# Hybrid attention and MLP trunk on one core: keys and queries split two heads at once, their halves placed by transfers inside SBUF

## The chip, the cores and the metric

The kernel runs on one core of a Trainium2 chip. Its engines work side by side, each through its own list of instructions in order: TensorE (PE, matmuls and transposes), VectorE (DVE), ScalarE (ACT), GpSimd (POOL), and SyncE (SP), which issues all transfers (DMAs) of this kernel. The metric is the time of one execution on the device in microseconds (us), as the median of several runs.

## What is computed

Two layers (DEPTH = 2) on x of 512 rows and 1024 columns, in float32. Each layer projects the normalised x once and hands the parts to three groups of attention heads of width 64; their outputs go through one output projection, and a gated MLP with a short causal convolution follows. Cut to what the change touches:

```python
FOX_HEADS, NSA_HEADS, NSA_KV_GROUPS, DIL_HEADS, HEAD_DIM = 4, 8, 2, 4, 64
proj = h @ w_in
(fq, fk, fv, ff, nq, kc, vc, ks, vs, kw, vw, ng, dq, dk, dv) = jnp.split(proj, splits, axis=-1)
o_fox = fox_attention(heads(fq, 4), heads(fk, 4), heads(fv, 4), log_f)
o_nsa = nsa_attention(rope(nq, 8), rope(kc, 2), heads(vc, 2), rope(ks, 2), heads(vs, 2),
                      rope(kw, 2), heads(vw, 2), gates, ...)
o_dil = dilated_attention(rope(dq, 4), rope(dk, 4), heads(dv, 4))
mix = concatenate([o_fox, o_nsa, o_dil], axis=-1);  return mix @ w_out
# within each: s = einsum('bqhd,bkhd->bhqk', q, k) * 64 ** -0.5, masked softmax, times v
```

## The kernel before

**Numbers.** A float32 value goes into PE as two parts in the format F32R: `hi`, the rounded value, and `lo`, the rest. A product is hi·hi + hi·lo + lo·hi. ACT writes hi (a copy into an F32R tile), DVE writes lo (value minus hi).

**Layout of scores.** A head has 64 columns, the array 128 rows. A tile `q` [128, 2 heads, 512 positions] holds for each head hi in partitions 0 to 63 and lo in 64 to 127. A tile `k` [128, 2, 512] belongs to one head: `k[:, 0]` holds hi twice, in both halves of the partitions, `k[:, 1]` lo twice. So two matmuls over 128 partitions make a score block from all parts.

**How they come about.** A projection leaves 128 positions x 64 columns per head in PSUM. `staged(...).evac` (L717 on) brings each of four position blocks into a row tile `r` (with `rope`, which rotates 16 of the 64 columns); for keys (`dup`) it writes every head twice side by side. `turn` (L735) turns a 128-column strip of the four row tiles with four PE transposes into one PSUM tile `pt` of [128, 512]: for queries two heads above each other, for keys one head twice. One step later `keep` calls the split: `q_evac` (ACT L485, DVE L486, once per head, 64 partitions each) or `k_evac` (ACT L492, DVE L493, 128 partitions, once per head). For the forgetting heads' keys `fk` the turning (`t_block`, L476) and the split stand in one line of their own. `fq` needs no turning: its split reads the projection's accumulator.

**Stages of a layer.** fq, fk, fv are projected first; then 96 attention units run (16 of the group f, 64 of n, 16 of d), and between them pieces of the other projections: nq (8 heads in two halves, nq0 and nq1), ks and kw (2 heads each, nks and nkw), kc and vc for the compressed keys, dq, dk, dv. The order on PE is written out by hand in program order: each unit's nine stages lie a fixed number of units apart (`LAGS`), `step()` issues the next piece, `budget` spreads the pieces over the units, and `operands(u)` calls `until(...)`, which issues pieces until the unit's q and k exist. The other engines' lists are ordered by a scheduler. Weights come through `load` (L134, SP) into one of few `raw` buffers per weight and are split by ACT (L148) and by DVE or POOL (L150).

**Buffers.** Row tiles `r` come from a pool of 10, q and k from a pool of 24 (`b`). PSUM has 2 buffers `pt`, 3 `acc`, 2 `s`, 1 `o`: a `pt` is free for the next transposes when both split operations have read it.

Of the kernel before, what the change touches and what calls it, by code (L numbers as in the profile page):

```python
# [10 lines left out]
F32R = mybir.dt.float32r  # L11
I32 = mybir.dt.int32
AF = mybir.ActivationFunctionType
ALU = mybir.AluOpType
# [60 lines left out]
def tile_hybrid_block(  # L75
# [6 lines left out]
    nc = tc.nc  # L82
# [12 lines left out]
    def nm(p):  # L95
        uid[0] += 1
        return f"{p}_{uid[0]}"

    def ps(tag):
        return psum.tile([128, 512], F32, tag=tag, bufs=PSB[tag], name=nm(tag))  # L100

    def bt(shape, dt=F32, name="b"):
        return big.tile(shape, dt, tag="b", name=nm(name))

    def rt(shape=(128, 512), dt=F32):
        return rowp.tile(list(shape), dt, tag="r", name=nm("r"))
# [4 lines left out]
    def f(ap):  # L111
        return ap.bitcast(F32)
# [4 lines left out]
    def bc(ap, axis, n):  # L117
        a = ap.unsqueeze(axis)
        shape = list(a.shape)
        shape[axis] = n  # L120
        return a.to_broadcast(shape)
# [322 lines left out]
    for l in range(DEPTH):  # L444
# [5 lines left out]
        def s_mms(o, s, ks, w, first, last):  # L450
            sl = slice(128 * s, 128 * s + 128)
            n = len(ks)
            ks = list(ks)
            order = sorted(range(n), key=lambda i: KORDER.index(ks[i]))
            for z, i in enumerate(order):
                k, i = ks[order[z]], order[z]
                mm(o, HH(k)[:, sl], w[0][:, i], first and z == 0, False)
                mm(o, HH(k)[:, sl], w[1][:, i], False, False)
                mm(o, HL(k)[:, sl], w[0][:, i], False, last and z == n - 1)
# [15 lines left out]
        def t_block(tiles, c0):  # L475
            p = ps("pt")  # L476
            for s in range(NST):
                nc.tensor.transpose(p[:, 128 * s:128 * s + 128], tiles[s][:, c0:c0 + 128], ident)
            return p
# [8 lines left out]
            return q  # L488

        def k_evac(p):  # L490
            k = bt([128, 2, 512], F32R, "k")
            nc.scalar.activation(k[:, 0, :], p, AF.Copy)  # L492
            nc.vector.tensor_sub(k[:, 1, :], p, f(k[:, 0, :]))  # L493
            return k

        def new_v(nh=2):
            return bt([128, 8 // nh, nh, 2, 64], F32R, "v")
# [6 lines left out]
        def hd(ap):  # L504
            return ap.rearrange("p (h d) -> p h d", d=64)

        store = {}
        sl256 = lambda pp, s: pp[s // 2][:, 256 * (s % 2):256 * (s % 2) + 256]
# [7 lines left out]
        pk_ = [ps("acc"), ps("acc")]  # L516
        fv = [new_v(4), new_v(4)]
        tl = []
        tmode = tc.manual_schedule(engines={mybir.EngineType.PE})
        tmode.__enter__()  # L520
        for s in range(NST):
            if s % 2 == 0:
                for c in range(2):
                    for u in range(s, s + 2):
                        s_mms(sl256(pk_, u), u, range(4 * c, 4 * c + 4), wk[c], c == 0 and u % 2 == 0,
                              c == 1 and u % 2 == 1)
            p = ps("s")[:, 0:284]
            for c, (k0, k1) in enumerate(((0, 3), (3, 6), (6, 8))):
                s_mms(p, s, range(k0, k1), wv[c], c == 0, c == 2)
            if s == 1:  # L530
                turn_pair(1, 0, l, HT2)
            v_evac(fv[s // 2], s % 2, p[:, 0:256])
            nc.vector.tensor_add(zz[:, s, :], p[:, 256:284], bias)
            d = rt((128, 4, 2, 64))
            nc.scalar.activation(d, bc(hd(sl256(pk_, s)), 2, 2), AF.Copy)
            tl.append(d.rearrange("p h u d -> p (h u d)"))
        tmode.__exit__(None, None, None)
        store["fv"] = fv
        store["fk"] = [k_evac(t_block(tl, 128 * j)) for j in range(4)]
        cpar = small.tile([128, 2, 88], F32, tag="cpar", bufs=1, name=nm("cpar"))  # L540
        crow = rt((88, 2, 128))
        for j in range(3):
            d = crow[44 * (j % 2):44 * (j % 2) + 44, j // 2, :]
# [66 lines left out]
        if l == 0:  # L610
# [20 lines left out]
            for v, lg in ((2.0, -math.log(2.0)), (3.0, -math.log(3.0))):  # L631
                t = rt()
# [86 lines left out]
        def staged(key, turned, dup, nh, v=None, plain=0):  # L719

            tl = []

            def evac(s, p):
                w = nh * 64 * (2 if dup else 1)
                d = rt((128, w + plain))
                rope(d[:, 0:w].rearrange("p (h u d) -> p h u d", h=nh, d=64), hd(p[:, 0:64 * nh]), s, nh)
                if plain:
                    nc.scalar.activation(d[:, w:w + plain], p[:, 64 * nh:64 * nh + plain], AF.Copy)
                if v is not None:
                    if s == 0:  # L730
                        store[v] = new_v()
                    v_evac(store[v], s, p[:, 64 * nh:64 * nh + 128])
                tl.append(d)

            def turn(j):  # L735
                p = ps(TT)
                for s in range(NST):
                    nc.tensor.transpose(p[:, 128 * s:128 * s + 128], tl[s][:, 128 * j:128 * j + 128], ident)  # L738
                pieces.later(EV[3], keep, p)

            def keep(p):
                store.setdefault(key, []).append((k_evac if dup else q_evac)(p))

            return evac, [(turn, j) for j in range(nh * (2 if dup else 1) // 2)]

        def dv_evac(s, p):
            if s == 0:
# [325 lines left out]
        def until(key, n=1):  # L1073
            while len(store.get(key, ())) < n and (live[0] or pieces.late):
                step()


        units = []
# [5 lines left out]
        def operands(u):  # L1084
            h, gq = u["h"], u["h"] // 4
            if u["grp"] in "fd":
                g = u["grp"]
                for key, n in ((g + "q", h // 2 + 1), (g + "k", h + 1)):
                    until(key, n)
                vt = store[g + "v"]  # L1090
                return (store[g + "q"][h // 2][:, h % 2, :], store[g + "k"][h],
                        lambda b: vt[b // 2][:, b % 2, h].rearrange("p u d -> p (u d)"), cmask if g == "f" else dmask, None)
            kk, vv = (("nks", "vs"), ("nkw", "vw"))[u["br"]]
            until("nq", h // 2 + 1)
            until(kk, gq + 1)
            vt = store[vv]
            return (store["nq"][h // 2][:, h % 2, :], store[kk][gq],
                    lambda b: vt[:, b, gq].rearrange("p u d -> p (u d)"), cmask, 3 * h + 1 + u["br"])

        state, whole = {"o": None, "p": None}, []  # L1100

        def st_scores(u):
            t = u["t"]
            n = u["n"] = 128 * (t + 1)
            q, k, u["v"], u["mask"], u["gate"] = operands(u)
            if t != 1:
                state["s"] = ps("s")
            S = u["S"] = state["s"][:, 128 * (t == 1):]
            qs = q[:, 128 * t:128 * t + 128]
            fox = u["grp"] == "f"  # L1110
            mm(S[:, 0:n], qs, k[:, 0, 0:n], t != 1, False)
            mm(S[:, 0:n], qs, k[:, 1, 0:n], False, not fox)
            if fox:
                mm(S[:, 0:n], esel[:, u["h"], :], cst[:, 0:n], False, True)
# [122 lines left out]
        with tc.manual_schedule(engines={mybir.EngineType.PE}):  # L1237
            for i in range(FIRST):
                step()
            for i in range(len(units) + LO):  # L1240
                slot[0] = i
                U = lambda lag: units[i - lag] if 0 <= i - lag < len(units) else None
                for lag, fn in stages:
                    if U(lag) is not None:
                        fn(U(lag))
                budget += 1.4 if i < 12 else max(NPIECES - pieces.n, 0.8) / max(len(units) - i, 1)
                while budget >= 1.0:
                    budget -= 1.0
                    if live[0] or pieces.late:
                        step()  # L1250
                chain_step()
                if store.get("pc") and whole and whole[0][1] <= i:
                    cmp_values(whole.pop(0)[0])
            while whole or live[0] or pieces.late:
                if whole and store.get("pc"):
                    cmp_values(whole.pop(0)[0])
                elif live[0] or pieces.late:
                    step()
                    chain_step()
            for s in range(2):  # L1260
                mid_load(s)
            ws = [getw(l, "up", 0, n, ahead=0) for n in range(2)]
# [69 lines left out]
        for i in range(11):  # L1332
# [3 lines left out]
            for c in range(2):  # L1336
                cd = []
                for b in range(2):
                    n = 2 * c + b
                    if i > 0:  # L1340
                        w = getw(l, "up", i, n)
                        p = ps(tg[n])
                        up_mms(p, w, slice(0, 512), True, True)
                    else:
                        p = pts[n]
# [77 lines left out]
```

## Time and profile before

| what | us |
|---|---|
| median of 3 runs (lowest to highest) | 1369.35 (1369.28 to 1370.27) |
| the profiled execution: its own time | 1369.22 |
| its span, first to last instruction | 1367.4 |
| PE busy in the span | 1337.2 |
| DVE / ACT / POOL busy | 853.2 / 730.3 / 277.7 |

The profile is of one execution. Its page lists the busy time of each engine; further views list single instructions by start time (the timeline), groups of instructions by line, stretches of the span, the waits of an engine by what ended them, and the transfers with the time from issue to landing. Matmuls are pipelined: the start of the next one tells more of a matmul's cost than its own duration. Both layers run through the same stages, the first from about 18 to 690 us.

### The profile page before, as it was taken

To read this page: it belongs to the slowest core of one execution; us is meant where nothing else is said; L and a number is where in the kernel's file an instruction comes from. 1 tells how busy PE (TensorE), PEld (TensorE's weight loads), DVE (VectorE), ACT (ScalarE), POOL (GpSimd) and SP (SyncE) were. 2 spreads that over 40 slices of the span, in tenths; PEclk is the share of its full clock that TensorE was granted. 3 is DMA by queue.
4 is the path that set the end of the run, shared out by engine and by line. 5 is a ranking of instruction groups with operands and counts; after the bars stand their busy time and mean duration, and the time that the engine had idled before them with its cause. 6 is when DMAs were issued, how large, how long until landed. Compare 5 with 4: busy or idle time off the path is not lost.

```text
span 1367.4 us, 21035 instructions
## 1 busy us (share of the span) xinstructions
PE 1337.2 (98%) x7855; PEld 1177.4 (86%) x7855; DVE 853.2 (62%) x1901; ACT 730.3 (53%) x1516; POOL 277.7 (20%) x335
## 2 busy tenths in 40 slices
PE   9999999999999999999999999999999999999997
PEld 8899898988888888888898998899898888888886
DVE  7677878768655555433464877787776555554334
ACT  6567867777533333333465677677774333333232
POOL 1364663331000000000004646543210000000000
PEclk9999999999999999999999999999999999999999
DMA  6323311141333333323323242101423333332231
GB/s 181 94 63 117 90 32 47 42 160 32 108 93 98 103 93 95 101 98 123 111 89 100 63 139 63 32 32 47 154 63 99 102 93 93 105 96 93 94 122 62
DMA packets 145519, 123.75 MB, mean 91 GB/s; under 512 B 8264, under 2 KB 135688, under 8 KB 145416
## 3 DMA queue, kind: packets, MB, share of 16 engines
q1 hardware_dynamic: 145416, 122.40, 29.6%
q8 instruction: 62, 1.02, 0.3%
q14 instruction: 41, 0.34, 0.1%
HBM read 118.19 MB, written 4.19 MB: 90 GB/s over the span
## 4 chain that ended last, share of the span: by engine, by line
PE 83%; DVE 6%; ACT 5%; POOL 4%; issue 2%; DMA 0%; SPq 0%; ACTq 0%; POOLq 0%; DVEq 0%
PE acc L115 38%; PE s L115 19%; PE pt L115 12%; PE o L115 10%; PE pt L1155 3%; PE pt L738 1%; DVE hl L267 1%; POOL wt L796 1%; POOL r L1142 1%; POOL wl_dq L150 1%; POOL wl_dv L150 1%; ACT hh L266 1%; DVE x L914 0%; DVE r L1125 0%; DVE pl L1171 0%
## 5 line engine op out<-in xcount | busy, mean ns | idle before, releaser
L150 DVE TENSOR_TENSOR wl_up<-raw_up,wh_up 128x1024 fp32r<-128x1024 f32 x78 | 95.5, 1225 | 170.9 <-ACT wh_up L148 170.9
L148 ACT ACTIVATE wh_up<-raw_up 128x1024 fp32r<-128x1024 f32 (+1 forms) x90 | 89.4, 1002 | 160.5 <-PE acc L115 68.2
L150 DVE TENSOR_TENSOR wl_wd<-raw_wd,wh_wd 128x1024 fp32r<-128x1024 f32 x42 | 51.5, 1225 | 133.7 <-ACT wh_wd L148 133.7
L148 ACT ACTIVATE wh_wd<-raw_wd 128x1024 fp32r<-128x1024 f32 x42 | 44.5, 1060 | 144.8 <-PE pt L115 135.5
L1130 ACT ACTIVATE r<-r,sm 128x128 f32<-128x128 f32 x192 | 107.0, 558 | 15.5 <-DVE sm L1125 14.6
L1142 POOL TENSOR_SCALAR r<-r,sm,gates 128x128 f32<-128x128 f32 (+3 forms) x128 | 82.4, 652 | 111.1 <-DVE sm L1138 71.3
L115 PE MATMUL acc<-hh,wl_up 128*128 128x512 f32 (+1 forms) x272 | 102.4, 377 | 0.0
L115 PE MATMUL acc<-hl,wh_up 128*128 128x512 f32 (+1 forms) x272 | 102.4, 376 | 0.0
L115 PE MATMUL acc<-hh,wh_up 128*128 128x512 f32 (+1 forms) x272 | 102.4, 376 | 0.0
L1171 DVE TENSOR_TENSOR pl<-pt,ph 128x384 fp32r<-128x384 f32 x144 | 85.5, 596 | 19.8 <-ACT ph L1166 18.1
L115 PE MATMUL s<-k,q 128*128 128x512 f32 (+3 forms) x384 | 96.8, 338 | 0.0
L150 POOL TENSOR_TENSOR wl_kc<-raw_kc,wh_kc 128x512 fp32r<-128x512 f32 x8 | 11.6, 1471 | 417.5 <-ACT wh_kc L148 416.7
L1166 ACT ACTIVATE ph<-pt 128x384 fp32r<-128x384 f32 x144 | 75.0, 523 | 25.1 <-PE pt L1155 24.0
L1125 DVE CUSTOM_DVE_ANT_0 r<-s,cmask 128x128 f32<-128x128 f32 (+3 forms) x160 | 75.6, 481 | 16.3 <-PE s L115 10.4
L115 PE MATMUL acc<-wh_wd,gh 128*128 128x512 f32 x252 | 83.8, 389 | 0.0
L1155 PE MATMUL pt<-ident,r 128*128 128x128 f32 x480 | 77.7, 276 | 5.5 <-DVE k L493 2.4
L115 PE MATMUL s<-hh,wh_up 128*128 128x512 f32 (+1 forms) x224 | 80.4, 359 | 0.0
L115 PE MATMUL s<-hl,wh_up 128*128 128x512 f32 (+1 forms) x224 | 80.4, 359 | 0.0
L115 PE MATMUL s<-hh,wl_up 128*128 128x512 f32 (+1 forms) x224 | 80.4, 359 | 0.0
L1347 ACT ACTIVATE r<-r 128x512 f32<-128x512 f32 x44 | 27.8, 632 | 85.8 <-DVE r L1328 85.5
L1155 PEld LDWEIGHTS pt<-ident,r 128*128 128x128 f32 x480 | 55.3, 140 | 15.3 <-issue 5.4
L115 PE MATMUL acc<-wh_wo,mix 128*128 128x256 f32 (+1 forms) x296 | 67.4, 305 | 0.0
(438 smaller groups left out, 4115.5 us busy)
## 6 DMA issues: line engine op xcount, KB each, us to landing
raw_up<-in_w_up_dram SPq DMA_DIRECT2D x88, 512.0 KB, 3.8
raw_wd<-in_w_down_dram SPq DMA_DIRECT2D x44, 512.0 KB, 3.4
raw_wo<-in_w_out_dram SPq DMA_DIRECT2D x16, 512.0 KB, 3.4
x<-in_x_dram SPq DMA_DIRECT2D x8, 512.0 KB, 6.2
raw_nq<-in_w_in_dram SPq DMA_DIRECT2D x8, 512.0 KB, 3.6
raw_w<-in_cmp_w_k_dram SPq DMA_DIRECT2D x8, 512.0 KB, 4.2
raw_w<-in_cmp_w_v_dram SPq DMA_DIRECT2D x8, 512.0 KB, 4.4
raw_fk<-in_w_in_dram SPq DMA_DIRECT2D x4, 512.0 KB, 5.8
```

Source lines behind the costliest of these rows:

```text
L115: nc.tensor.matmul(o, lhsT=lhsT, rhs=rhs, start=start, stop=stop, skip_group_check=True)
L148: nc.scalar.activation(cutting(hi, a, e), cutting(raw, a, e), AF.Copy)
L150: (nc.gpsimd if pool else nc.vector).tensor_sub(cutting(lo, a, e), cutting(raw, a, e), cutting(f(hi), a, e))
L266: nc.scalar.activation(hi, src, AF.Copy, scale=gain[:, k:k + 1])
L267: nc.vector.scalar_tensor_tensor(lo, src, gain[:, k:k + 1], f(hi), op0=ALU.mult, op1=ALU.subtract)
L1125: nc.vector.tensor_tensor_reduce(row[:, 0:n], u["S"][:, 0:n], u["mask"][:, 512 - n:512], op0=ALU.add, op1=ALU.min, scale=1.0, scalar=3.0e3 ...
L1130: nc.scalar.activation(row[:, 0:n], row[:, 0:n], AF.Exp, scale=-1.0, bias=sm_[0], accum_out=sm_[1])
L1142: nc.gpsimd.tensor_scalar(row[:, 0:n], row[:, 0:n], z["sm"][2], g_, op0=ALU.mult, op1=ALU.mult)
L1155: nc.tensor.transpose(p[:, 128 * c:128 * c + 128], blocks[z], ident)
L1166: nc.scalar.activation(hi, src, AF.Copy)
L1171: nc.vector.tensor_sub(*u["lo"])
L1347: nc.scalar.activation(cd[0], cd[0], AF.Silu)
```

## The change

`k_evac` gets a PSUM tile with two different heads, one above the other. ACT and DVE split both at once into a tile `k[1]`, which then has both heads' hi and lo, but each in one half of the partitions alone. Three transfers inside SBUF, issued by SP, put them in place: the first head's half goes into both halves of a second tile `k[0]`, then the second head's half goes into the lower half of `k[1]`, over the first head. `q_move` takes the place of `q_evac` for turned queries: hi and lo of two heads go into two row tiles, and four transfers bring the quarters into `q`. Keys are no longer written twice into their row tiles, so half as many strips are turned. `ask` calls `operands` for the next unit, one unit earlier than its scores, so that turns come a unit earlier.

```diff
         def k_evac(p):
-            k = bt([128, 2, 512], F32R, "k")
-            nc.scalar.activation(k[:, 0, :], p, AF.Copy)
-            nc.vector.tensor_sub(k[:, 1, :], p, f(k[:, 0, :]))
+
+            k = [bt([128, 2, 512], F32R, "k") for _ in range(2)]
+            own, other = slice(64, 128), slice(0, 64)
+            nc.scalar.activation(k[1][:, 0, :], p, AF.Copy)
+            nc.vector.tensor_sub(k[1][:, 1, :], p, f(k[1][:, 0, :]))
+            for h in (other, own):
+                nc.sync.dma_start(f(k[0])[h], f(k[1])[other])
+            nc.sync.dma_start(f(k[1])[other], f(k[1])[own])
             return k
+
+        def q_move(p):
+
+            hi, lo = rt(dt=F32R), rt(dt=F32R)
+            nc.scalar.activation(hi, p, AF.Copy, scale=-0.125)
+            nc.vector.scalar_tensor_tensor(lo, p, -0.125, f(hi), op0=ALU.mult, op1=ALU.subtract)
+            q = bt([128, 2, 512], F32R, "q")
+            for j in range(2):
+                for i, part in enumerate((hi, lo)):
+                    nc.sync.dma_start(f(q)[64 * i:64 * i + 64, j, :], f(part)[64 * j:64 * j + 64, :])
+            return [q]
...
-            d = rt((128, 4, 2, 64))
-            nc.scalar.activation(d, bc(hd(sl256(pk_, s)), 2, 2), AF.Copy)
-            tl.append(d.rearrange("p h u d -> p (h u d)"))
+            d = rt((128, 256))
+            nc.scalar.activation(d, sl256(pk_, s), AF.Copy)
+            tl.append(d)
         tmode.__exit__(None, None, None)
         store["fv"] = fv
-        store["fk"] = [k_evac(t_block(tl, 128 * j)) for j in range(4)]
+        store["fk"] = [k for j in range(2) for k in k_evac(t_block(tl, 128 * j))]
...
-                w = nh * 64 * (2 if dup else 1)
+                w = nh * 64
...
-                store.setdefault(key, []).append((k_evac if dup else q_evac)(p))
-
-            return evac, [(turn, j) for j in range(nh * (2 if dup else 1) // 2)]
+                store.setdefault(key, []).extend((k_evac if dup else q_move)(p))
+
+            return evac, [(turn, j) for j in range(nh // 2)]
...
+        def ask(u):
+            if u["t"] == 0 and u["grp"] != "f":
+                operands(u)
...
+                if i + 1 < len(units):
+                    ask(units[i + 1])
```

In all 48 transposes go from PE's list, and 84 transfers come into SP's, 36 of 256 KB for keys and 48 of 128 KB for queries. ACT and DVE have 12 key splits each instead of 24, and 12 turned-query splits instead of 24. Three places of the new order follow; the number in a name counts the tiles and differs between the two kernels.

The first place is PE's list at the turn of nq0 in the first layer. Before, from the last projection matmul of kw (`acc`) over the second turn of queries to the first scores of the branch kw/ks (`s`, from `k` of nks and `q` of nq0):

```order
L115 MATMUL acc_1526<-wh_kw_229_1366,hl_94 128x256
L738 MATMUL pt_1599<-ident,r_1418 128x128 [waits PE_49]
L738 MATMUL pt_1599<-ident,r_1450 128x128
L738 MATMUL pt_1599<-ident,r_1499 128x128
L738 MATMUL pt_1599<-ident,r_1547 128x128
L115 MATMUL s_1609<-k_1342,q_1604 128x128 [waits DVE_49]
L115 MATMUL s_1609<-k_1342,q_1604 128x128
L115 MATMUL acc_1526<-wh_kw_229_1366,hh_89 128x256
```

And the same place now, where `q_1577` is filled by transfers from the first turn, which stands 12 projection matmuls ahead of these rows in both kernels:

```order
L115 MATMUL acc_1495<-wh_kw_227_1357,hl_94 128x256
L754 MATMUL pt_1568<-ident,r_1406 128x128
L754 MATMUL pt_1568<-ident,r_1438 128x128
L754 MATMUL pt_1568<-ident,r_1487 128x128
L754 MATMUL pt_1568<-ident,r_1516 128x128
L115 MATMUL s_1582<-k_590,q_720 128x512 x2
L115 MATMUL s_1582<-cst,esel 128x512
L1176 MATMUL pt_1596<-ident,r_1383 128x128 [waits DVE_49,Pool_49]
L1176 MATMUL pt_1596<-ident,r_1383 128x128 x3
L115 MATMUL s_1601<-k_1329,q_1577 128x128 [waits DMAHW5_49,DMAHW4_49,DMAHW7_49,DMAHW0_49,DVE_49]
L115 MATMUL s_1601<-k_1329,q_1577 128x128
```

Scores of the last forgetting unit (`s_1582`) and a turn of probabilities (`pt_1596`) have come between the turn and the first score that reads the new q, and this score now waits for transfers (DMAHW) instead of DVE.

The second place is PE's list at the turn of nkw. Before, from the last matmul of the compressed values (`acc`, second weight `w1`) on:

```order
L115 MATMUL acc_1876<-wl_w_1_0_326_1842,wth_1384 128x256
L738 MATMUL pt_1893<-ident,r_1745 128x128
L738 MATMUL pt_1893<-ident,r_1770 128x128
L738 MATMUL pt_1893<-ident,r_1802 128x128
L738 MATMUL pt_1893<-ident,r_1826 128x128
L115 MATMUL s_1901<-k_1898,q_1604 128x128 [waits Activation_49]
L115 MATMUL s_1901<-k_1898,q_1604 128x128 [waits DVE_49]
L115 MATMUL acc_1838<-wh_nq_0_317_1812,hh_89 128x256
```

And now, again with 8 matmuls of `acc` between the (now only) turn and the first row:

```order
L115 MATMUL acc_1854<-wl_w_1_0_322_1820,wth_1375 128x256
L115 MATMUL s_1878<-k_1329,q_1577 128x512 x2
L1176 MATMUL pt_1891<-ident,r_1605 128x128 x4
L115 MATMUL s_1896<-k_1871,q_1577 128x128 [waits DMAHW3_49,DMAHW2_49,DVE_49]
L115 MATMUL s_1896<-k_1871,q_1577 128x128
L115 MATMUL acc_1816<-wh_nq_0_313_1790,hh_89 128x256
```

The second turn is gone, one score block and one turn of probabilities stand in its place, and the first score with the new k waits for two transfers.

The third place is SP's list at nkw. Before, it holds weight loads alone:

```order
L134 DMA raw_w_1_2_357_2001<-in_cmp_w_v_dram 128x4x256 [waits DMAHW4_49,DVE_49]
L134 DMA raw_w_1_3_364_2029<-in_cmp_w_v_dram 128x4x256 [waits DMAHW5_49,DVE_49]
L134 DMA raw_dv_385_2122<-in_w_in_dram 128x4x256 [waits DMAHW6_49,Pool_49]
L134 DMA raw_dv_417_2256<-in_w_in_dram 128x4x256 [waits DMAHW7_49,DVE_49]
L134 DMA raw_dq_436_2320<-in_w_in_dram 128x4x256 [waits DMAHW0_49,DVE_49]
```

And now:

```order
L134 DMA raw_w_1_3_364_2021<-in_cmp_w_v_dram 128x4x256 [waits DMAHW6_49,DMAHW1_49,DVE_49]
L497 DMA k_1871<-k_1872 64x1024 [waits DMAHW2_49,DVE_49]
L497 DMA k_1871<-k_1872 64x1024 [waits DMAHW3_49]
L134 DMA raw_dv_389_2126<-in_w_in_dram 128x4x256 [waits DMAHW7_49,Pool_49]
L498 DMA k_1872<-k_1872 64x1024 [waits DMAHW3_49,DMAHW2_49]
L134 DMA raw_dv_417_2248<-in_w_in_dram 128x4x256 [waits DMAHW0_49,DVE_49]
```

Two transfers that wait for DVE's split come ahead of the load of dv, and the third, which waits until the first two have landed, behind it.

## Rows read from the trace of the kernel before

**Rows 1.** The page, busy time and share of the span, instructions of each engine.

```profile
PE 1337.2 (98%) x7855; PEld 1177.4 (86%) x7855; DVE 853.2 (62%) x1901; ACT 730.3 (53%) x1516; POOL 277.7 (20%) x335
```

**Rows 2.** Stretches: length, busy us of each engine (instructions), granted clock, DMA share, GB/s.

```profile
92.00:132.00 40.00, 39.89 (x318) 38.59 (x319) 31.17 (x92) 30.49 (x75) 16.03 (x21) 1.00 0.38 118
132.00:172.00 40.00, 37.74 (x288) 35.52 (x287) 31.73 (x98) 31.45 (x82) 26.82 (x31) 1.00 0.30 85
172.00:212.00 40.00, 37.63 (x295) 35.38 (x293) 30.51 (x107) 25.85 (x73) 22.64 (x34) 1.00 0.13 41
```

**Rows 3.** PE's waits, whole run: what waited, for whom, total us, times, longest.

```profile
PE pt L738 <- DVE q L486: 2.5, 2, 1.3
PE pt L1155 <- DVE k L493: 2.4, 2, 1.2
...
PE pt L115 <- DVE r L351: 1.5, 1, 1.5
...
PE pt L548 <- DVE k L493: 0.9, 1, 0.9
...
PE pt L1155 <- DVE q L486: 0.6, 2, 0.3
PE acc L115 <- DVE q L486: 0.5, 1, 0.5
```

**Rows 4.** PE's timeline around turned blocks: start us, length us, instruction, count.

```profile
43.44 0.48 PE L115 MATMUL acc<-hh,wl_fq 128*128 128x512 f32 x1
43.76 0.60 PE L478 MATMUL pt<-ident,r 128*128 128x128 f32 x4
44.11 0.48 PE L115 MATMUL acc<-hh,wh_fq 128*128 128x512 f32 x1
...
93.76 0.28 PE L115 MATMUL acc<-wl_nq,hh 128*128 128x256 f32 x1
93.88 0.28 PE L115 MATMUL acc<-wh_nq,hl 128*128 128x256 f32 x1
94.10 0.66 PE L738 MATMUL pt<-ident,r 128*128 128x128 f32 x4
94.52 0.71 PE L115 MATMUL s<-k,q 128*128 128x512 f32 x2
```

**Rows 5.** Timeline at the first turn of nq0, PE, ACT and DVE.

```profile
109.94 0.62 ACT L148 ACTIVATE wh_kw<-raw_kw 128x512 fp32r<-128x512 f32 x1
...
109.97 0.36 PE L115 MATMUL acc<-wh_kw,hh 128*128 128x256 f32 x1
...
110.46 0.58 ACT L485 ACTIVATE q<-pt 64x512 fp32r<-64x512 f32 x1
...
111.07 0.68 DVE L486 SCALAR_TENSOR_TENSOR q<-pt,q 64x512 fp32r<-64x512 f32 x1 [0.84 <-ACT q L485]
...
111.85 0.42 PE L115 MATMUL s<-k,q 128*128 128x128 f32 x2
```

**Rows 6.** Transfers: count, KB each, us to landing; then one issue on SP's timeline.

```profile
raw_up<-in_w_up_dram SPq DMA_DIRECT2D x88, 512.0 KB, 3.8
...
out_dram<-x SPq DMA_DIRECT2D x4, 512.0 KB, 2.6
...
w2r<-in_cmp_w_k_dram SPq DMA_DIRECT2D x2, 64.0 KB, 2.0
...
113.62 0.37 SPq L134 DMA_DIRECT2D raw_nq<-in_w_in_dram  x1
```

**Rows 7.** Timeline at the first turn of nkw, PE, ACT and DVE.

```profile
129.13 0.36 PE L115 MATMUL acc<-wh_w,wth 128*128 128x256 f32 x1
...
129.40 0.60 ACT L492 ACTIVATE k<-pt 128x512 fp32r<-128x512 f32 x1 [0.25 <-PE pt L738]
...
130.02 0.69 DVE L493 TENSOR_TENSOR k<-pt,k 128x512 fp32r<-128x512 f32 x1 [0.28 <-ACT k L492]
...
130.51 0.58 PE L115 MATMUL s<-k,q 128*128 128x128 f32 x2
```

## The prediction

> **What bounds the kernel now.** First the busy shares of the page: TensorE (PE) is busy for 1337.2 us of the 1367.4 us span, VectorE (DVE) for 62%, ScalarE (ACT) for 53% [rows 1]. So only two things count: matmul time that disappears, and time in which PE stands still. Second the stretches in which the changed work lies: from 92 to 132 us PE is busy 39.89 of 40 us, from 132 to 172 only 37.74, from 172 to 212 only 37.63, at a granted clock of 1.00 [rows 2]. In the first there is no idle time to win back and none in which a new delay could hide; the other two have 2.3 and 2.4 us. Third the list of what PE waited for: after the splits of keys (k, L493) and queries (q, L486) it stood for 2.4, 0.9, 2.5, 0.6 and 0.5 us in the whole run [rows 3]. The two layers run alike, so what I find in the first counts twice. The profiled run took 1369.22 us, 1.8 more than its span and 0.1 less than the median of 1369.35; I add to 1369.2.
>
> **Part 1: transposes that go.** Keys of a pair of heads came out of two blocks of four transposes and now come out of one. Per layer 6 of 12 blocks go (fk 2, ks 1, kw 1, dk 2), 12 in all. A transpose is shown with 273 ns, but they overlap, so I take what a block adds to the spacing of its neighbours. At 93.88 the spacing without a block is 0.12; with one it is 0.64, so 0.52. At 43.44 two 128x512 matmuls stand 0.67 apart; they take twice the columns, some 0.23, so the block costs 0.44 [rows 4]. 12 x 0.48 = 5.8 us gone from PE, ends 5.3 and 6.2.
>
> **Part 2: ACT and DVE work that goes.** 12 pairs of k splits and as many of q, some 0.58 + 0.68 us a pair [rows 5], and half the width of the doubled key rows. That is some 30 us off two engines that are not the bound, so it counts only where PE waited for it: the five waits above without the 2.5 make 4.4 us. dk (2.4) should go whole, since two of four splits per layer vanish. Of the other 2.0 I keep one half, because another buffer may be next. I take -3.4, ends -2 and -4.4.
>
> **Part 3: transfers on the path, query side (nq0).** Before, a turned block is split straight into q and the scores start right behind. Now hi and lo go to two row tiles, and four transfers carry them into q. In the first turn, matmuls go on at 109.97, ACT begins the first split at 110.46 and DVE at 111.07, and the scores start at 111.85 with no wait [rows 5]. In the new order 12 projection matmuls, four transposes, three 128x512 matmuls and four more transposes stand between the turn and the first score that needs q: 12 x 0.12 + 0.42 + 3 x 0.23 + 0.42 = 2.97, so PE is there at 112.9. ACT's split comes behind both halves of wh_kw (109.94 and a second one; 0.52 apart by the start of the next), so at about 111.0; DVE follows 0.61 later and needs 0.68: lo is ready at 112.3 and its transfer is issued at 112.35. What a transfer inside SBUF takes no row shows. The shortest landing in the trace is 2.0 (a 64 KB load), the one transfer that starts in SBUF and met little traffic took 2.6 for 512 KB, the big loads 3.8 [rows 6]. These are the bounds. The new transfers are of 128 and 256 KB with rows of 2 and 4 KB, the latter as in the 2.6 row; I take 2.3 for q, 2.6 for k. Lo lands at 114.65, PE starts 0.05 later: a stall of 1.8 per layer, 3.6 in all, ends 3.0 and 6.6.
>
> **Part 4: transfers on the path, key side (kw).** Before: turn over at 129.13, ACT at 129.40, DVE 130.02 to 130.71, scores from 130.51 [rows 7]. In the new order 8 matmuls, two 128x512 matmuls and four transposes stand between: 0.96 + 0.46 + 0.42 = 1.84, PE is there at 131.0. The score reads k of the first head, which is filled by two transfers, both behind DVE at 130.71; SyncE (SP) issues them one after the other, at 130.75 and, by the 0.37 of one issue [rows 6], 131.1. The second lands at 133.7: a stall of 2.75 per layer, 5.5 in all, ends 4.3 and 7.9. This is the dearest term, and PE had nothing to spare there.
>
> **Part 5: the rest.** The third k transfer waits on SP until both others have landed, and queued behind it stand weight loads. At kw it even stands behind a load; its first reader is the second head, whole rounds of matmuls later. At fk, ks, dq and dk the new order has far more matmuls between turn and first reader (dk, the shortest, some 9 us of them by the spacings above) than landing takes: nothing, though a load queued there behind a waiting transfer goes out up to 2 us later. At nq1 PE stood 1.3 for L486 [rows 3], since both q splits and a chain of small DVE work stood ahead. Now DVE does the small work first: the second turn starts some 0.7 earlier, but the lo split and what follows come later. The same work stands on DVE, so I take 0, ends -1.4 and +3. The long stalls of parts 3 and 4 let DVE and POOL catch up, so a little of the 4.6 us of idle time per layer that follow [rows 2] should go: -0.6, ends 0 and -4.6 (half of it).
>
> **Sum.** -5.8 - 3.4 + 3.6 + 5.5 + 0 - 0.6 = -0.7, or 1368.5 us.
>
> **A page against the row.** No row shows a transfer that touches only 64 partitions. The Trainium skill, SBUF — State Buffer, section "Door 1: The DMA port swizzle", says that such a transfer reaches only half of the 16 ports and that two of them do not add up to a full one. With the figures of its curve (about 2 us fixed, then the ports' rate of some 218 GB/s) I estimate 256 KB at 3.2 us and the second of two at 4.4 after the first issue, which would make the kw stall 4.2 and the sum about +2. It is the mechanism of the second rival below, which is priced from rows.
>
> **Rivals.**
> (a) Faster. Transfers land in 2.0, as the shortest load [rows 6], and half of the idle time from 132 to 212 us comes back, 2.3 per layer [rows 2], because the waits there are for DVE and POOL, which gain time in each stall. -5.8 - 3.4 + 3.0 + 4.3 - 4.6 = -6.5, 1362.7. For it: most of PE's waits are of this kind. Against: at kw and nq0 PE has no idle time, and the engines' chains there start from PE.
> (b) Slower: the landing decides. From the 64 KB load to the 512 KB load the landing grows by 1.8 [rows 6], so by 1.0 for 256 KB. If half the partitions mean half the rate, a k transfer lands 1.0 later, and the second, behind the first, 1.0 to 2.0; I take 1.5: a kw stall of 4.25, 8.5 in all. A q transfer has half the bytes, 0.5: 4.6 in all. With 1 us at nq1 for row tiles that come free later: -5.8 - 3.4 + 4.6 + 8.5 + 1 - 0.6 = +4.3, 1373.5. The sum crosses zero when the four stalls are 0.2 longer than I take, and the kernel is slower by 0.2% when they are 0.85 longer (landing of 3.2 for q, 3.5 for k). For it: loads in this trace do take 3.8. Against: the 2.6 row.
> (c) The clock falls. PE's longest wait among those listed is 1.5 us [rows 3], and the clock was 1.00 [rows 2]; a stall of 2.75 or more is longer than any of these. If matmuls worth as much time as the stall then ran at 1.2 instead of 2.4 GHz, each kw stall would cost 2.75 more: +5.5, 1374. TensorE: Matmul & The Clock Gate of the Trainium skill says in Part 1 that the clock halves after an idle time; no row here shows at which stall.
> (d) It does not do what it says: the blocks of fk and dk, 8 of 12, stand where PE waits for the splits anyway, so that blocks and waits can't both be won. Then 3.8 is lost: 1372.3. Against: the dk wait is 1.2 per layer at one place only.
>
> **How the numbers follow.** The forecast, 1368.5 (its own range 1366.6 to 1371.2), has a chance of 0.42; (a) 0.28; (b) 0.19; (c) 0.04; (d) 0.07. The bound between same and faster or slower is 0.2%, 2.7 us, about what a measurement of this kernel can tell from no change. Faster: (a) and a bit of the forecast, 0.30. Slower: (b), (c) and most of (d), 0.28. Same: 0.42. With 1 in 10 left out on each side the range reaches from 1362, just beyond (a), to 1375.5, beyond (b) and (c): terms 3 to 5 have ends that make these.
>
> **What would show it.** In the profile after: PE waits for DMA at the scores (L115) of about 1.8 (q) and 2.75 (k), two of each; no wait behind the k split at dk; PE's busy time 5 to 6 us less; landing of the new transfers 2.3 and 2.6. I am wrong if these land in under 1.7 or over 3.3, if PE's idle time after 132 us falls by more than 1 us per layer apart from the new stalls, or if the granted clock falls below 1.00 at 131 us.

## The result: 11 us slower

The changed kernel takes 1380.61 us as the median of five runs (1379.89 to 1381.84), the kernel before 1369.42 beside it: a ratio of 1.0081 with a 95% interval of 1.0067 to 1.0096. The forecast was 1368.5 with a range of 1362 to 1375.5, so both the time and its side of the kernel before are missed. The profiled run took 1381.15 us, its span is 1379.4. One of the seven runs of the kernel with kw undone, further down, was in a slow state (4276.8 us) and is left out of its median; no other number here is of a slow run.

The page of the changed kernel, busy time, share of the span and instructions, answers to [rows 1]:

```profile
PE 1336.5 (97%) x7807; PEld 1178.9 (85%) x7807; DVE 837.8 (61%) x1877; ACT 713.4 (52%) x1492; POOL 278.6 (20%) x335
```

48 transposes are gone, yet PE is busy for as long as before (1336.5 for 1337.2): what is left takes longer. DVE and ACT lost some 16 us each. Where the time went is told by the stretches, as [rows 2] (length, busy time of PE, PEld, DVE, ACT, POOL, granted clock, DMA share, GB/s):

```profile
92.00:132.00 40.00, 37.36 (x298) 36.09 (x296) 28.67 (x84) 27.09 (x68) 16.07 (x19) 1.00 0.62 165
132.00:172.00 40.00, 34.47 (x247) 32.80 (x247) 23.46 (x78) 24.68 (x67) 23.49 (x29) 0.91 0.36 95
172.00:212.00 40.00, 37.13 (x285) 35.83 (x286) 30.61 (x106) 27.06 (x76) 20.96 (x30) 0.96 0.23 62
```

Two things are new. PE stands longer, in the first two stretches above all (2.64 and 5.53 us, before 0.11 and 2.26), and the granted clock, 1.00 in all three before, is 0.91 and 0.96 in the last two. What PE waited for, as [rows 3] (total us, times, longest):

```profile
PE s L115 <- DMA k<-k: 9.9, 2, 5.4
PE pt L1176 <- DVE pl L1192: 4.5, 2, 2.3
PE pt L754 <- DVE pl L1192: 2.9, 4, 1.0
PE pt L1176 <- DVE k L495: 2.4, 2, 1.2
...
PE s L115 <- DVE r L505: 1.6, 1, 1.6
...
PE s L115 <- DVE sm L1159: 1.4, 1, 1.4
```

The scores of nkw wait for the transfers of the keys, 5.4 and 4.5 us. The last two rows are the scores of nq0, one per layer. They name DVE, but the low half was split by 109.93 us in the first layer and these scores began at 112.55; the transfer that carries it landed at 112.31 by the trace's semaphore records (792.69 and 792.89 in the second layer), so these are waits for the queries' transfers. The wait behind the k split at dk, 2.4 in both layers together, is still there. The stall at nq1 has another releaser (L1192, the low part of turned probabilities). The transfers, as in [rows 6]:

```profile
k<-k SPq DMA_DIRECT2D x36, 256.0 KB, 4.3
q<-r SPq DMA_DIRECT2D x48, 128.0 KB, 2.3
```

The timeline at nkw answers to [rows 7]; SP's issues stand in it:

```profile
128.30 0.37 SPq L134 DMA_DIRECT2D raw_w<-in_cmp_w_v_dram  x1
128.31 0.73 PE L754 MATMUL pt<-ident,r 128*128 128x128 f32 x4
129.08 0.60 ACT L494 ACTIVATE k<-pt 128x512 fp32r<-128x512 f32 x1 [0.25 <-PE pt L754]
129.71 0.69 DVE L495 TENSOR_TENSOR k<-pt,k 128x512 fp32r<-128x512 f32 x1
...
130.34 0.60 PE L1176 MATMUL pt<-ident,r 128*128 128x128 f32 x4
130.43 1.11 SPq L497 DMA_DIRECT2D k<-k  x2
...
136.23 0.46 SPq L498 DMA_DIRECT2D k<-k  x1
...
136.31 0.66 PE L115 MATMUL s<-k,q 128*128 128x128 f32 x2 [5.37 <-DMA k<-k]
```

PE is ready at 130.9, as forecast (131.0), and the transfers are issued from 130.43, as forecast (130.75). By the trace's semaphore records the second, issued at 130.95, lands at 136.17: 5.2 us after its issue instead of 2.6. Then the clock, in short stretches with the same columns:

```profile
130.00:134.00 4.00, 0.94 (x7) 0.56 (x5) 2.03 (x6) 2.66 (x7) 3.27 (x4) 1.00 1.02 257
134.00:136.00 2.00, 0.00 (x0) 0.00 (x0) 0.00 (x0) 0.00 (x0) 0.60 (x1) 0.54 0.68 156
136.00:138.00 2.00, 1.69 (x8) 1.73 (x9) 0.00 (x0) 0.00 (x0) 0.00 (x0) 0.50 0.82 243
138.00:140.00 2.00, 2.00 (x11) 2.00 (x11) 0.00 (x0) 0.00 (x0) 0.00 (x0) 0.50 0.27 57
140.00:142.00 2.00, 2.00 (x15) 2.00 (x14) 1.20 (x5) 1.26 (x5) 0.00 (x0) 0.75 0.00 0
...
144.00:146.00 2.00, 2.00 (x19) 1.86 (x17) 1.94 (x5) 1.97 (x5) 0.00 (x0) 1.00 0.19 24
...
174.00:178.00 4.00, 1.73 (x15) 1.32 (x13) 3.58 (x12) 2.99 (x7) 1.69 (x3) 1.00 0.57 131
178.00:180.00 2.00, 2.00 (x14) 2.00 (x13) 1.55 (x5) 1.41 (x3) 0.66 (x1) 0.64 0.85 196
180.00:182.00 2.00, 2.00 (x11) 2.00 (x11) 0.00 (x0) 1.15 (x2) 1.68 (x2) 0.51 0.29 67
```

While PE stands, the clock falls to half (at 134.2 us), and it stays at half for about 4.7 us after PE has begun again at 136.3: 11 matmuls from 138 to 140 us, where 19 stand from 144 to 146. DVE and ACT stand as well, because they wait for PE. A second fall comes at 178.5 us, after the stall at nq1, and lasts 3.4 us. In each layer there are 10.2 us at half clock (6.8 and 3.4), 20.4 of 1379.

Put side by side by the first matmuls with the same weights, the changed kernel is 2.2 us ahead of the kernel before when kw's projection begins (106 us), about level at 121, 7.7 behind at 137, 9.9 behind when dv's second weights begin (171), and 7.4 behind at the end of the first attention (268).

### The profile page after: what moved, and what is told of

Same layout as the page of the kernel before. It is cut to its first block, busy times and chain, and to the rows that moved or that the text cites. A ratio compares the mean times of both kernels' runs of the same rounds, so it can differ in the third digit from the quotient of the medians.

```text
span 1379.4 us, 21142 instructions
## 1 busy us (share of the span) xinstructions
PE 1336.5 (97%) x7807; PEld 1178.9 (85%) x7807; DVE 837.8 (61%) x1877; ACT 713.4 (52%) x1492; POOL 278.6 (20%) x335
## 4 chain that ended last, share of the span: by engine, by line
PE 82%; DVE 8%; ACT 5%; POOL 2%; issue 2%; DMA 1%; SPq 0%; DVEq 0%; ACTq 0%; POOLq 0%
PE acc L115 38%; PE s L115 19%; PE pt L115 12%; PE o L115 10%; PE pt L1176 3%; DVE hl L267 1%; DMA k<-k 1%; DVE r L1146 1%; POOL wt L812 1%; ACT r L1151 1%; DVE wt L812 1%; ACT hh L266 1%; PE pt L754 0%; DVE pl L1192 0%; DVE x L930 0%
## 5 line engine op out<-in xcount | busy, mean ns | idle before, releaser
L1192 DVE TENSOR_TENSOR pl<-pt,ph 128x384 fp32r<-128x384 f32 x144 | 85.7, 596 | 16.9 <-ACT ph L1187 15.9
L1176 PE MATMUL pt<-ident,r 128*128 128x128 f32 x480 | 77.8, 277 | 6.9 <-DVE pl L1192 4.5
L115 PEld LDWEIGHTS s<-k,q 128*128 128x128 f32 x384 | 59.6, 195 | 18.6 <-issue 12.5
L1176 PEld LDWEIGHTS pt<-ident,r 128*128 128x128 f32 x480 | 56.1, 141 | 15.0 <-POOL r L1163 5.3
```

What stands on the lines that cost most here:

```text
L115: nc.tensor.matmul(o, lhsT=lhsT, rhs=rhs, start=start, stop=stop, skip_group_check=True)
L1176: nc.tensor.transpose(p[:, 128 * c:128 * c + 128], blocks[z], ident)
L1192: nc.vector.tensor_sub(*u["lo"])
```

## The experiments

Three explanations stood against each other: A, the stall at nkw and the slow clock behind it (with some loss at nq1); B, the transfers alone, with a clock that costs nothing; C, the route of the queries.

**Keys alone.** The queries' split as before (`q_same` calls `q_evac`; all queries are staged with `new=False`), the keys as changed. The line that chooses:

```diff
-                store.setdefault(key, []).extend((k_evac if dup else q_move)(p))
+                store.setdefault(key, []).extend((k_evac if dup else (q_move if new else q_same))(p))
```

> Only the keys are split two heads at once; turned queries are split straight into q as before. Theory A (three causes: the stall at nkw while k's transfers land, the clock that falls behind it, and the stretch at nq1): this keeps the first two, 4.9 + 2.4 us per layer, and the gains of fewer transposes (5.8) and dk/fk waits (3): 1369.4 - 8.8 + 14.5 = about 1375. Rival B (the k transfers alone make the whole loss): about 1380. Rival C (the loss is in the row tiles of the queries): below 1368.

Measured: 1377.53 us (1375.73 to 1379.71), ratio 1.0060 (1.0045 to 1.0075). The keys make most of the loss, 8.1 us, more than theory A's 6 and less than B's 11. The stall at nkw is there in both layers, 4.7 and 4.3 us:

```profile
PE s L115 <- DMA k<-k: 9.0, 2, 4.7
```

**Queries alone.** The keys' rows doubled again and split once per head (`k_same`; all keys are staged with `new=False`, and fk calls it too). The line that chooses:

```diff
-                store.setdefault(key, []).extend((k_evac if dup else q_move)(p))
+                store.setdefault(key, []).extend(((k_evac if new else k_same) if dup else q_move)(p))
```

> Only the queries go through row tiles and transfers; keys keep their doubled rows and one split per head. Theory A: nq0's stall of some 2 us and nq1's loss of 2.2 us per layer, with a short fall of the clock behind nq1: about +7, 1376. Rival B: within 2 us of the kernel before, 1369 to 1371. Rival C: all of the loss, 1380.

Measured: 1370.80, ratio 1.0011 (1.0001 to 1.0020). A's 1376 is wrong here, and B's 1369 to 1371 is right: the queries alone cost 1.4. So C is out. The waits of PE and two stretches of this kernel:

```profile
PE pt L1183 <- DVE pl L1199: 4.5, 2, 2.3
PE pt L761 <- DVE pl L1199: 3.1, 4, 1.0
PE s L115 <- DMA q<-r: 2.5, 2, 1.3
...
132.00:172.00 40.00, 36.24 (x276) 34.05 (x275) 30.26 (x98) 30.40 (x81) 28.19 (x34) 1.00 0.38 105
172.00:212.00 40.00, 38.93 (x313) 37.53 (x312) 30.56 (x108) 27.38 (x76) 22.81 (x32) 1.00 0.18 54
```

The nq1 stall of 2.3 is there as in the changed kernel, but in this run the clock stays at 1.00, and the stretch gives the time back. It is not so in every run: five of the ten, the profiled one among them, had a mean granted clock of 0.999 and took 1369.95 to 1370.24; the other five had 0.997 and took 1371.36 to 1372.34. So the same stall is followed by a slow clock in some runs and not in others. 8.1 and 1.4 make 9.5, some 2 less than 11.2; the second fall of the clock in each layer, which neither half has in its profile, fits that, but was not tried by itself.

**A busy PE during the stall.** Matmuls whose result the real scores overwrite, in front of nkw's first scores:

```diff
+            if u["grp"] == "n" and u["br"] == 1 and u["h"] == 0 and t == 0:
+                other = store["nks"][0]
+                for j in range(20):
+                    mm(S[:, 0:512], other[:, 0, 0:128], other[:, 0, :], True, True)
```

> The change, and in front of the first scores that need nkw's keys 20 matmuls of 512 columns whose results are overwritten (some 4.6 us, shorter than the stall of 4.5 to 5.4 that stands there), so that PE does not stand still. Theory A: the clock stays at 1.00 from 132 to 172 us, where it fell to 0.50 for 6.8 us, of which PE worked some 4.7 us at half speed: 2.35 per layer are won, 4.7 in all, about 1376; the second fall, behind nq1, stays. Rival D (the low clock costs nothing, since DVE and ACT would have been waited for instead): unchanged, 1380 to 1381.

Measured: 1376.27 (1373.91 to 1378.25), ratio 1.0050 (1.0034 to 1.0067): 4.3 less than the changed kernel, though 20 matmuls were added; each of its four runs is below each of the five of the changed kernel. The stretches of its profile:

```profile
130.00:134.00 4.00, 4.00 (x22) 3.30 (x21) 1.82 (x6) 2.44 (x7) 3.49 (x4) 1.00 0.93 252
134.00:136.00 2.00, 1.28 (x6) 0.74 (x4) 0.00 (x0) 0.00 (x0) 0.45 (x1) 1.00 0.63 165
136.00:138.00 2.00, 1.89 (x16) 1.92 (x17) 0.00 (x0) 0.00 (x0) 0.00 (x0) 1.00 0.85 239
...
172.00:212.00 40.00, 37.39 (x289) 36.07 (x288) 29.19 (x101) 26.76 (x73) 22.44 (x31) 0.96 0.20 54
```

The keys take as long to land as before (4.4 us in the median), but the clock stays at 1.00 around 136 us. So the slow clock is a cost of its own, and B is out. The fall behind nq1 is still there in this layer (0.96): it does not need the one at nkw.

**One transfer over all partitions.** The first two transfers of a pair replaced by one of the same bytes; the upper half of `k[0]` then holds the other head's keys:

```diff
-            for h in (other, own):
-                nc.sync.dma_start(f(k[0])[h], f(k[1])[other])
+            nc.sync.dma_start(f(k[0]), f(k[1]))
```

> The change, with the first two transfers of each pair of keys replaced by one of 128 partitions and 512 KB (the same bytes; the upper half of k[0] then holds the other head, so the scores of one head in two are wrong, the work is the same). Theory A (a transfer that touches 64 partitions runs at half rate: its 4096-byte packets took some 310 ns where those that touch all partitions took 159): the packets are done in 1.3 instead of 2.5 us and one issue (0.5) falls away, so the stall at nkw is 1.3 to 1.8 shorter, about 3.2, and the clock falls less or not at all: 1380.6 - 3 without and - 8 with the clock, 1372.6 to 1377.6. Rival F (the landing is long because two weight loads are queued ahead, or because of what follows the last packet): stall of 4.5 to 5.4 as before, 1380.

Measured: 1377.12, ratio 1.0053 (1.0038 to 1.0068), 3.5 less than the changed kernel. From PE's waits and the stretches:

```profile
PE s L115 <- DMA k<-k: 7.4, 2, 3.8
...
132.00:172.00 40.00, 36.98 (x266) 34.81 (x266) 25.95 (x87) 26.41 (x71) 23.53 (x30) 0.96 0.35 97
```

The stall is 1.25 us shorter per layer, just under what half the packet time and one issue less were to give (1.3 to 1.8), and the clock is low for half as long there (3.4 us for 6.8). So the 64 partitions are one part of the long landing, not all of it: 3.7 is left where 2.75 was forecast for two transfers. Weight loads are another part. In the changed kernel two of 512 KB were issued at 126.7 and 128.3, and by the packet records 190 of their packets still moved after the first packet of the keys (131.6 us, 1.2 after its issue). From the durations of the packets I estimate 0.7 us of the 16 DMA engines' time for these and 2.3 for the keys' 128; the last of the keys' ended at 135.4, and the landing was told at 136.2. No run without the loads was made.

**kw undone.** Everything as changed, except the keys of nkw, which take the old route:

```diff
-            ... proj256("kw", *staged("nkw", True, True, 2, "vw"))
+            ... proj256("kw", *staged("nkw", True, True, 2, "vw", new=False))
```

> The change undone for the keys of nkw alone: doubled rows, two turns and two splits of 128 partitions, no transfers there. Theory A (the nkw stall and the clock behind it are most of the loss): without 4.9 us of stall and some 2 us of slower clock per layer, 1380.6 - 14 = about 1367, and the granted clock 1.00 from 132 to 172 us. Rival J (the loss is spread over nq0, nq1 and nkw; the next stall takes its place): 1373 or more.

Measured: 1366.40 as the median of six runs (1364.30 to 1367.29), ratio 0.9971 (0.9959 to 0.9983), as theory A said. One turned block of the twelve in a layer turns a gain of some 3 us into a loss of 11.2. The clock is not 1.00 throughout, as A had it:

```profile
132.00:172.00 40.00, 36.25 (x269) 34.06 (x269) 30.11 (x98) 30.04 (x80) 27.10 (x33) 0.98 0.39 105
```

The fall behind nq1 begins inside this stretch, at 170 us. The runs of this kernel also give a price for the clock: those with a mean granted clock of 0.996 took 1366.9 to 1367.3, with 0.998 1365.4 and 1365.9, with 0.999 1364.3. In the profile, of a run with 0.996, the clock is low once in each layer for 3.4 us, so 3.4 us at half clock cost about 1.4 (an estimate), not the 1.7 of lost matmul time.

**More lead.** The change with `ask(units[i + 4])` in place of `ask(units[i + 1])`:

```diff
-                if i + 1 < len(units):
-                    ask(units[i + 1])
+                if i + 4 < len(units):
+                    ask(units[i + 4])
```

> The change, with the next operands asked for four units ahead of their scores instead of one: by the new order 8.2 us of matmuls lie between nkw's turn and its first score, 20 us at nq0. Theory A: the stalls at nq0 (1.6) and nkw (4.9) and the first fall of the clock (2.35) go in both layers: 1380.6 - 17.7 = about 1363, nq1's loss stays. Rival E (pieces that come earlier meet weights that are not there, or the idle time only moves): 1370 or more.

Measured: 1360.68 (1360.41 to 1361.34), ratio 0.9937 (0.9922 to 0.9951): 8.7 us faster than the kernel before, 20 faster than the change as made and better than theory A's 1363. No wait for a transfer is left in PE's list. The keys' landing and the stretches read:

```profile
k<-k SPq DMA_DIRECT2D x36, 256.0 KB, 4.5
...
92.00:132.00 40.00, 40.00 (x323) 39.16 (x322) 28.45 (x82) 27.52 (x68) 16.93 (x19) 1.00 0.71 192
132.00:172.00 40.00, 38.34 (x292) 35.99 (x291) 30.14 (x101) 30.48 (x85) 26.44 (x34) 1.00 0.43 116
172.00:212.00 40.00, 39.61 (x303) 37.02 (x302) 32.59 (x115) 27.38 (x77) 23.16 (x32) 1.00 0.08 27
```

The keys land no sooner (4.5 us), but 8 us of matmuls lie between nkw's turn and its first score. The clock is 1.00.

**Is it the order that wins?** The old splits throughout, asked for four units ahead:

> No part of the change but the asking, and that four units ahead: keys doubled and split per head, queries straight into q. Theory A: the earlier asking by itself wins only part of the waits behind q and k splits (2.5 + 2.4 + 0.6 us in the list of waits): 1366 to 1369, so that of the 8.7 us which the change wins with it at least 5 are the change's own. Rival G (the order is what wins): 1361 to 1363.

Measured: 1370.06, ratio 1.0001 (0.9992 to 1.0011). The order alone wins nothing, less than expected; all of the 9.4 us between this kernel and the last are the change's own.

The old splits asked for one unit ahead:

> No part of the change but the asking one unit ahead. Theory A: the moved turns cost or win little: 1369 to 1371. Rival K (the new order alone loses at nq0 and nq1, where the lag grew by 2 us each): 1373 or more.

Measured: 1369.83, ratio 1.0000 (0.9991 to 1.0009). `ask` costs nothing either.

**What the transposes are worth.** The lead of four, with each transpose of a block of keys issued twice (here in `turn`; for fk the same in `t_block`):

```diff
+                    if dup:
+                        nc.tensor.transpose(p[:, 128 * s:128 * s + 128], tl[s][:, 128 * j:128 * j + 128], ident)
```

> The change asked for four units ahead (1360.7), with every transpose of a block of keys issued twice, so that as many stand in PE's list as before the change (48 more). Theory A: they cost 12 x 0.48 = 5.8 us, as read from the spacing: 1366.5. Rival H (hidden in waits of PE for other engines): under 2 us, 1361 to 1363.

Measured: 1363.66, ratio 0.9955 (0.9939 to 0.9972). 48 more transposes cost 3.0 us, 0.25 a block, between A's 5.8 and H's under 2. PE's line of the page with 4.1 us more than the 1331.9 of the lead of four:

```profile
PE 1336.0 (98%) x7855; PEld 1177.2 (86%) x7855; DVE 833.1 (61%) x1877; ACT 711.2 (52%) x1492; POOL 280.0 (21%) x335
```

They were doubled in place; blocks that stand alone may cost a little more, which was not tried.

**Keys alone, with lead.**

> Keys alone two heads at once, queries straight into q, asked for four units ahead. Theory A: the queries' transfers win nothing on PE, so without them the nq1 stretch is as before and the time is within 1.5 us of 1360.7. Rival I (the row tiles and the two split operations instead of four win at nq1 too): 1363 or more.

Measured: 1362.25, ratio 0.9945 (0.9930 to 0.9960), 1.6 above the full change, just past the 1.5 that A allowed and short of rival I's 1363; the runs of the two do not overlap (1362.02 to 1362.33, and 1360.41 to 1361.34). With lead the queries' route gains some 1.6 us, on which engine was not taken apart.

**fk alone.** The kernel before, with the change for the forgetting heads' keys only:

> The kernel before with the change for the forgetting heads' keys alone (fk, four heads, two blocks, six transfers per layer), which have long until their first score. Theory A: 8 of the 24 transposes per layer go at the 0.06 us each that 48 doubled ones cost (3.0 in all), and fk's waits (0.9 + 0.5) with them: 1366 to 1367.5. Rival L (nothing of this reaches the end): 1369.

Measured: 1366.30, ratio 0.9975 (0.9965 to 0.9985), 3.3 us won where nobody waits for the landing, as expected.

**More lead still.**

> The change, asked for six units ahead instead of four. Theory A: at four no stall for a transfer is left, so more lead wins nothing: 1360 to 1361.5. Rival M (later waits shrink further): under 1359.5.

Measured: 1364.86, ratio 0.9965 (0.9952 to 0.9978): slower than with four, against both theories. PE's waits in its profile:

```profile
PE pt L1176 <- DVE sm L1159: 5.2, 6, 1.2
PE acc L1054 <- DVE sm L1046: 2.7, 2, 1.3
...
172.00:212.00 40.00, 37.72 (x282) 35.62 (x282) 29.79 (x103) 25.04 (x71) 20.18 (x29) 0.96 0.11 33
```

In the stretches from 132 to 212 us PE stands 5.5 us (3.21 and 2.28), with four units 2.05, and at the head of the list are softmax rows (sm). The clock falls once in the profile, for 3.4 us in the first layer, which by the price above is not most of the 4.2. That pieces drawn further ahead leave other places with too little matmul work fits these rows; it was not tried.

## Why the prediction was wrong

**Part 1, the transposes: sign right, half the size.** 5.8 was forecast, 3.0 measured. The spacing of two neighbours of one block was taken for its price, 0.44 to 0.52; blocks doubled in place show 0.25.

**Part 2, ACT and DVE work: too small as a whole, wrong in its piece.** dk's 2.4 "should go whole" and is still there (L1176 behind L495). But with the stalls out of the way the change wins 9.4 us, 3.0 of them by transposes; so some 6.4 come from splits and waits where 3.4 were forecast. fk alone gives 3.3. How the rest divides was not taken apart.

**Part 3, nq0: right.** Landing of q 2.3 as forecast; the stall is 1.6 and 1.4 (the rows of L505 and L1159 in the waits) where 1.8 was forecast, and 1.3 in the kernel with queries alone.

**Part 4, nkw: the step that failed.** Where PE would be and when the transfers go out came out within 0.4 us. The landing did not: 2.6 was taken from the 512 KB that go out at the end with little beside them, and was 5.2 here, 4.3 in the median. The stall was 5.4 and 4.5, not 2.75, together 4.4 us more. The packet records of the trace show 4096-byte packets of the keys here at 307 ns in the median (252 at nkw in the second layer), where those of other transfers took 159: about half rate, as rival (b) had it, and one transfer over all partitions took 1.25 off the stall. The estimate from the Trainium skill (SBUF — State Buffer, "Door 1: The DMA port swizzle") thus came nearer than the sum: a landing 4.4 after the first issue and a stall of 4.2, where 5.7 and 5.4 were measured. The packets of two loads in the way were in neither.

**Part 5.** nq1 was forecast at 0 with ends of -1.4 and +3. PE stands 2.3 there once per layer, but the queries alone, with that stall and with nq0's 1.3 per layer, cost 1.4 in all. So nq1 can't have cost much as long as the clock holds; by itself it was not measured.

**The clock, rival (c): given 0.04, and it came.** Its mechanism was named: a stall longer than any that the trace of before shows. Its price was set at 5.5 in all; the forecast itself put the clock at nothing. At the 1.4 per 3.4 us that the runs show, the 20.4 us of the changed kernel, less some 4.5 inside the stalls, make some 6.5 (an estimate); 4.3 came back when PE was kept busy at nkw alone. So the size was near and the chance was the error: nothing in the trace of before spoke for the clock to hold through a stall longer than any in it. What it would have done at the 2.75 that were forecast stays open; the stalls at nkw in these runs are 3.6 us or longer (0.8 at most where PE was kept busy).

**The sum in the end.** From the kernel before: -9.4 (the change without stalls, from the kernels with a lead of four), +9.9 (nkw), +3.0 (nq0) and some 6.5 for the clock make 10.0; the last 1.2 of the 11.2 measured was not taken apart. The kernel with kw undone fits: the change is 14.2 slower than it, and the stall at nkw (9.9) with the clock behind it (some 3.7 at the same price) makes 13.6. The forecast's gain, 9.8 with the later idle time, came near the 9.4 by luck: the transposes were 2.8 too much and the splits and waits 3.0 too little. The nkw stall was too small by 4.4, the clock was at nothing, and these two are the miss.

## What to carry to other kernels

A transfer that replaces engine work has to be issued its landing time, not its packet time, ahead of the reader; find the reader's distance in the order of the bound engine, and move the producer before replacing the work. Here three more units of lead turn +11 us into -9. Price such a transfer by its partitions and by the loads that are queued at that moment, and not by the fastest row of the trace. And a stall of PE is not priced by its length alone: if it is longer than any that the trace shows at full clock, count the slow matmuls behind it.

## What the hardware showed that was not expected

- The clock fell to half while PE stood for 5.4 us, and also behind the row of shorter waits around nq1 in the changed kernel (PE busy for 4.73 of 8 us, 170 to 178); in the profiled run with the queries alone, the stall of 2.3 at the same place left it at 1.00.
- The fall behind nq1 needs none at nkw ahead of it: without the nkw transfers it is in the profile once per layer, and with PE kept busy at nkw in the first layer alone. Nor is it in every run: with the queries alone, half of the ten runs show the lower clock.
- SP takes 0.46 to 0.59 us in the median to issue a transfer inside SBUF, and 0.48 for the one over all 128 partitions, where a load takes 0.37.
- 256 KB inside SBUF took 4.3 us to land in the median, longer than 512 KB of a weight from memory (3.8, [rows 6]).
